# Weight splits and modulation products in instructions of 512 columns in place of 1024, in a kernel of four transformer blocks

## The chip, the cores and the metric

The kernel runs on one core of one Trainium2 chip. The metric is the device time of one execution in microseconds; the kernel before takes 1881.81 us, the median of three runs (1880.52 to 1883.42). The profile is of one more execution.

## The reference

Two models follow each other on one sequence of 512 tokens of width 1024, all in fp32, each of two layers. Each layer of both takes shift, scale and gate columns from a condition vector (the modulation), normalises the tokens, multiplies them with an input projection, mixes, multiplies with an output projection and adds the gated result; the second model has a wide MLP behind that.

```python
def modulation(cond, w_mod, b_mod):
    m = jax.nn.silu(cond) @ w_mod + b_mod
    return jnp.split(m, 3, axis=-1)
# first model: layer 0 pool mixer + attention, layer 1 Hyena convolutions + Fourier mixer
    h = rmsnorm(x, norm_g[i]) * (1 + scale) + shift
    ...
    x = x + gate * y
# second model, each of two layers l
    mod = cond @ w_mod[l] + b_mod[l]
    sh1, sc1, gt1, sh2, sc2, gt2 = [m[:, None, :] for m in jnp.split(mod, N_MOD, axis=-1)]
    h = rms_norm(x, norm_g[l, 0]) * (1.0 + sc1) + sh1
    y = mixer_block(h, ...)          # short conv, sparse attention, gated linear attention, gMLP
    x = x + gt1 * rms_norm(y, norm_g[l, 1])
    h = rms_norm(x, norm_g[l, 2]) * (1.0 + sc2) + sh2
    y = jnp.square(jax.nn.relu(h @ w_up[l])) @ w_down[l]
    x = x + gt2 * rms_norm(y, norm_g[l, 3])
```

## The kernel before, in words

Tokens lie along the columns: the state xT is 8 tiles of 128 features by 512 tokens and stays in SBUF. A projection with fp32 accuracy is made of three fp32r products: every operand is split in a part hi (rounded to fp32r by ScalarE) and a part lo (the rest, subtracted on VectorE), and mm3 (line 811) multiplies hi by hi, hi by lo and lo by hi into one PSUM bank.

**Weights.** wblock (line 795) brings in a block of 256 output columns: for each half of the contraction one DMA of 128x1024 (four k tiles of 256 columns side by side) into a ring of three "raw" tiles, one copy on ScalarE into hi and one subtraction on VectorE into lo, out of a ring of eight "wh" tiles, which makes four pairs. The first projection of the second model has blocks of other widths too (272, 268 and 128 columns, so tiles of 1088, 1072 and 512). Most blocks of the up projection go another way, winograd_fm (line 963), with splits of 512 columns of its own.

**Modulation.** All but two of the modulation vectors (16 of 1024 numbers) are made on VectorE by mod_cols (line 1159): the transposed weights come in as eight 128x1024 tiles in a ring of two ("mraw"); each is multiplied with the condition's row ("crow", the same on all partitions) and summed along the columns by one instruction into one column of the result. The profile shows such a product as CUSTOM_DVE_ANT_0 with a read-out of the sum, DVE_READ_ACCUMULATOR2_ANT, behind it. A generator "mods" hands these out between blocks; need(n) (line 1282) asks for them at the latest. The first two vectors ("m0", line 1240) come from TensorE at the start.

**Seams.** Where one projection ends and a norm must be known before the next begins, cross (line 926) works by halves of the tokens: the last output tiles ("tail"), the sums of squares, the reciprocal roots by rsqrt (line 1039, nine steps of two columns on VectorE, tiles "sa", twice in a sandwich of two norms), their broadcast by TensorE, the new input's tiles hi and lo by make_h (line 1126) on VectorE, ScalarE and POOL, and the first tiles of the next projection ("head"). There are such seams at L0out/L1norm, L1out/finN/nsa 0, wo/sand1/mlp in both layers, and mlp 0/sand2 0/nsa 1.

**Order.** Nothing is issued as it is written. Plan records each operation with its engine, a cost, the phase (pl.ph, such as "nsa 1" or "L1f") and its dependences, found from ranges of rows and columns of each buffer (record, line 202; box, line 110). schedule (line 298) then places all operations by a list: time after time it takes the engine and the ready operation that can start first, and among those that can start at that time on an engine the one with the greatest priority o.bl. That is made of the due time, counted back from TensorE's order, and a bias of the phase, in us (SCHED, line 30). wins limits, for a pool ("pg" pages of SBUF, "ps" banks of PSUM) and a phase, how far ahead of the oldest unfinished user a buffer may be taken, in us of TensorE's work; lead does the same for "mods". Some additions may go to VectorE or POOL as there is room. All transfers are issued by the SP queue in the order that the list gives. Every engine then runs its own list in order; emit (line 551, with the call at line 564) writes the instructions out, which is why nearly all rows have line 564, and are told apart by tile names.

Of the kernel before, what the change touches and what calls it, by code (L numbers as in the profile page):

```python
# [10 lines left out]
F32 = mybir.dt.float32  # L11
F32R = mybir.dt.float32r
I32 = mybir.dt.int32
AF = mybir.ActivationFunctionType
OP = mybir.AluOpType
# [2 lines left out]
P = 128  # L18
S = 512
HV = (slice(0, 256), slice(256, 512))  # L20
GA, GB, GC = 9,12,15
MY = 4
NF = 2
# [29 lines left out]
    },  # L53
    bias={
        "": -15, ("SP", "L1out"): 8, ("SP", "m0"): -30, "L0 gemm 0": -8, "L0 gemm 2": -8, "L0norm": 20,
        "L0out": -15, "L0q": 106, "L1 gemm 0": 265, "L1 gemm 1": 22, "L1f": 68, "L1norm": 270, "L1out": -7,
        "conv 0": 8, "ctx": 8, "end": 170, "finN": 67, "gla 1": -15, "gla chain 0": -32, "gla chain 1": -38,
        "gmlp 0": -15, "gmlp 1": -8, "gmlp chain 0": 30, "gmlp chain 1": 40, "head 0": 75, "head 4": 15,
        "hyena chain 1": 30, "hyena chain 2": 82, "mlp 0": -8, "mlp 1": -253, "mods": -45, "nsa 0": 8,
        "sand1 1": 8, "sand2 0": 210,  # L60
    },
)
D = 1024
# [88 lines left out]
class Plan:  # L152
# [145 lines left out]
    def schedule(self):  # L298
# [11 lines left out]
        if self.prio is None:  # L310
            t = 0.0
# [11 lines left out]
            for o in ops:  # L323
                o.bl = -self.prio[o.idx]
        for o in ops:
            o.bl += self.bias.get(o.ph, 0.0) + (self.bias.get(("SP", o.ph), 0.0) if o.eng == "SP" else 0.0)
        live = {p: np.zeros(n + 1, np.int32) for p in self.pools}
        for b in {id(b): b for o in ops for b in o.bufs}.values():
            live[b.pool][b.first:b.last + 1] += b.need
# [14 lines left out]
        pos, t = [], 0.0  # L344
# [94 lines left out]
        while left:  # L439
            pick, ps = None, 1e18  # L440
            top = max((o.bl for e in names[:4] for o in ready[e] if o.deps), default=0.0)
            for e in names:
# [10 lines left out]
                for o in pool:  # L453
# [9 lines left out]
                    if any(b.slot is None for b in o.bufs):  # L463
                        q = slots(o)
# [17 lines left out]
                if bs < ps:  # L482
                    pick, ps, pe = b, bs, e
# [4 lines left out]
            if pick is None:  # L488
                o = ops[front]
# [3 lines left out]
            o, e, s = pick, pe, ps  # L493
# [41 lines left out]
            for i in o.succ:  # L535
                q = ops[i]
# [171 lines left out]
def tile_two_blocks(ctx: ExitStack, tc: tile.TileContext, a, out):  # L708
# [48 lines left out]
    def small(n, dt=F32, tag=None):  # L757
        t = pl.alloc("sa" if n <= 16 else "sb", n)
        return t if dt == F32 else t.bitcast(dt)


    V, A, G, T = (pl.engs[n] for n in ("DVE", "ACT", "POOL", "PE"))
# [32 lines left out]
    def wblock(w, c0, nkt=KT, r0=0):  # L795

        name, l = w
        off, wd = IN_AT[c0] if name == "w_in_2" else (0, 256)
        hl = []
        for hh in range(r0 // 4, (r0 + nkt) // 4):  # L800
            src, hi, lo = wraw()[:, :4 * wd], wsplit().bitcast(F32R)[:, :4 * wd], wsplit().bitcast(F32R)[:, :4 * wd]
            if name == "w_in_2":
                D_(src, a[name][l, off + hh * 4 * P * wd:off + (hh + 1) * 4 * P * wd].rearrange("(p n) -> p n", p=P))
            else:
                D_(src, a[name][l, c0 // 256, hh])
            A.activation(hi, src, AF.Copy)
            V.tensor_sub(lo, src, hi.bitcast(F32))
            hl.append(tuple(t.rearrange("p (k n) -> p k n", k=4) for t in (hi, lo)))
        return hl

# [345 lines left out]
    crow = keep([P, D], "crow")  # L1156
    mraw = ring("mraw", 2, D)

    def mod_cols(i, dst):

        old, pl.ph = pl.ph, "mods"
        for t in range(KT):
            raw = mraw()
            D_(raw, a["wmT"][i, t])
            V.tensor_tensor_reduce(raw, raw, crow, 1.0, 0.0, OP.mult, OP.add, accum_out=dst[:, t:t + 1])
            if t % MY == MY - 1:
                pl.ph = old
                yield
                old, pl.ph = pl.ph, "mods"
        pl.ph = old  # L1170


# [69 lines left out]
    m0 = keep([P, 16, 2], "m0")  # L1242
    for j in range(2):
        pa = [mmt(), mmt()]
        for k in range(KT):
            for hh in range(2):
                raw = pg()
# [5 lines left out]
        ps = axt()  # L1253
# [228 lines left out]
    for gi in range(4):  # L1482
        o = (gi % 2) * 64
# [277 lines left out]
    for i in range(2):  # L1761
        fc = pg()
        D_(fc, a["cst_fchan"][:, i * S:(i + 1) * S])
        ps = axt()
# [14 lines left out]
    for m in range(2):  # L1779
# [6 lines left out]
        qs, yd = pg(), pg()  # L1786
# [584 lines left out]
    for l in range(2):  # L2371
# [5 lines left out]
        st, head = nsa_head(l, W, act)  # L2377
# [11 lines left out]
        t = convmix(l, W, act)  # L2389
# [115 lines left out]
    for j in range(4):  # L2505
        gr.append(hp())
        ps = axt()
# [71 lines left out]
```

## Time and profile before

| | |
|---|---|
| median of three runs | 1881.81 us |
| the profiled execution | 1881.66 us |
| its span, first to last instruction | 1879.8 us |
| TensorE (PE) busy, matmuls | 1815.2 us, 97% |
| VectorE (DVE) busy | 1548.7 us, 82% |
| ScalarE (ACT) busy | 1017.0 us, 54% |
| GpSimd (POOL) busy | 194.4 us, 10% |
| mean granted TensorE clock | 0.991 |
| HBM traffic | 129 GB/s over the span |

The page gives each engine's busy time, then the groups of instructions by tile names and shape. A window row gives the same for a stretch of time. A wait is idle time of an engine, put down to the instruction that ended it. In names of tiles, "raw" is a weight tile as loaded, "wh" a split one, "sa" a small tile of up to 16 columns, "pg" any page of 512 columns, "ps" a PSUM bank.

### The profile page before, as it was taken

The numbers are of one execution on the slowest core, as the hardware profiler recorded it, in microseconds if no ns is written. First come the engines' busy times: TensorE is split into PE (matmuls) and PEld (weight loads), VectorE is DVE, ScalarE is ACT, GpSimd is POOL, SyncE is SP. The second block draws the span as 40 slices with busy tenths as digits, with TensorE's granted clock in tenths as the row PEclk, the third lists the DMA queues.
The fourth block names the chain that finished last, engine by engine and source line by source line (L and its number), as shares of the span: only waits on it lengthen the run. The fifth ranks groups of instructions, "written<-read, shape, count | busy, mean of one in ns | idle before, by whom it ended". The sixth has DMA issues, their size and how long they took to land. (4 is left out here: it accounts for less than half of the span.)

```text
span 1879.8 us, 33476 instructions
## 1 busy us (share of the span) xinstructions
PE 1815.2 (97%) x12451; PEld 1630.2 (87%) x12451; DVE 1548.7 (82%) x3453; ACT 1017.0 (54%) x2100; POOL 194.4 (10%) x204
## 2 busy tenths in 40 slices
PE   5999999999999999999999999989999999999997
PEld 2798879988988988778888889988977889999997
DVE  6687997978998699787999867799968799766777
ACT  5565674543334566564664444575656457444455
POOL 0100000000221011011210000022201130000000
PEclk9999999999999999999999999999999999999999
DMA  7627443356433356311257422243541124222221
GB/s 235 224 79 241 146 141 113 112 176 223 156 120 124 111 174 213 113 46 46 79 168 233 160 102 101 91 160 126 181 155 41 50 79 147 101 91 101 102 90 68
DMA packets 92467, 245.29 MB, mean 130 GB/s; under 512 B 10443, under 2 KB 29167, under 8 KB 92048
## 3 DMA queue, kind: packets, MB, share of 16 engines
q1 hardware_dynamic: 92304, 243.15, 38.5%
q8 instruction: 98, 1.61, 0.4%
q14 instruction: 65, 0.53, 0.1%
HBM read 234.73 MB, written 8.39 MB: 129 GB/s over the span
## 5 line engine op out<-in xcount | busy, mean ns | idle before, releaser
L564 PE MATMUL ps<-pg,wh 128*128 128x256 f32 (+1 forms) x6336 | 1108.3, 328 | 7.4 <-ACT pg L564 4.7
L564 PEld LDWEIGHTS ps<-pg,wh 128*128 128x128 f32 x6336 | 919.1, 189 | 108.6 <-ACT pg L564 7.0
L564 PE MATMUL ps<-wh,pg 128*128 128x256 f32 (+2 forms) x2976 | 378.8, 283 | 5.0 <-ACT pg L564 5.0
L564 ACT ACTIVATE wh<-raw 128x1024 fp32r<-128x1024 f32 (+3 forms) x280 | 257.7, 923 | 231.6 <-PE ps L564 223.7
L564 PEld LDWEIGHTS ps<-wh,pg 128*128 128x128 f32 x2976 | 364.5, 189 | 8.8 <-ACT pg L564 6.1
L564 DVE TENSOR_TENSOR wh<-raw,wh 128x1024 fp32r<-128x1024 f32 (+3 forms) x280 | 297.7, 1066 | 66.7 <-ACT wh L564 51.5
L564 DVE TENSOR_TENSOR pg<-pg 128x256 f32<-128x256 f32 (+4 forms) x671 | 317.3, 508 | 37.6 <-ACT pg L564 33.3
L564 ACT ACTIVATE pg<-pg 128x256 f32<-128x256 f32 (+4 forms) x628 | 274.4, 472 | 128.3 <-DVE pg L564 75.0
L564 PE MATMUL ps<-pg 128*128 128x256 f32 (+7 forms) x1560 | 235.6, 300 | 7.5 <-DMA pg<-in_hy_w_dram 2.9
L564 DVE TENSOR_TENSOR pg<-pg,ps 128x256 f32<-128x256 f32 (+1 forms) x404 | 182.9, 473 | 59.7 <-PE ps L564 55.9
L564 PEld LDWEIGHTS ps<-pg 128*128 128x128 f32 (+4 forms) x1560 | 199.8, 184 | 33.8 <-issue 7.9
L564 POOL TENSOR_TENSOR pg<-pg 128x512 f32<-128x512 f32 (+4 forms) x96 | 114.7, 1199 | 908.9 <-ACT pg L564 488.0
L564 ACT ACTIVATE pg<-ps 128x512 fp32r<-128x512 f32 (+4 forms) x212 | 104.9, 524 | 116.2 <-PE ps L564 91.5
L564 DVE TENSOR_TENSOR pg<-ps,pg 128x512 f32<-128x512 f32 (+8 forms) x278 | 146.1, 561 | 26.1 <-ACT pg L564 20.6
L564 DVE CUSTOM_DVE_ANT_0 mraw<-mraw,crow 128x1024 f32<-128x1024 f32 x128 | 155.8, 1222 | 11.2 <-DMA mraw<-in_wmT_dram 11.2
L564 ACT ACTIVATE wh<-w 128x512 fp32r<-128x512 f32 x112 | 70.3, 630 | 127.3 <-PE ps L564 103.0
L564 ACT COPY pg<-ps 128x256 f32<-128x256 f32 (+5 forms) x184 | 78.3, 438 | 99.6 <-PE ps L564 96.9
L564 DVE TENSOR_TENSOR wh<-w,wh 128x512 fp32r<-128x512 f32 x112 | 77.0, 688 | 31.7 <-PE ps L564 19.5
L564 PE MATMUL ps<-ident,pg 128*128 128x128 f32 (+1 forms) x529 | 82.8, 276 | 5.0 <-ACT pg L564 1.8
L564 PEld LDWEIGHTS ps<-ident,pg 128*128 128x128 f32 (+1 forms) x529 | 63.1, 143 | 17.7 <-ACT pg L564 5.9
L564 ACT ACTIVATE pg<-ps,sa 128x512 f32<-128x512 f32 (+3 forms) x112 | 60.6, 553 | 28.8 <-DVE sa L564 27.0
L564 PE MATMUL ps<-pg,w 128*128 128x256 f32 (+1 forms) x408 | 68.0, 284 | 1.4 <-DVE pg L564 1.4
(138 smaller groups left out, 1127.1 us busy)
## 6 DMA issues: line engine op xcount, KB each, us to landing
mraw<-in_wmT_dram SPq DMA_DIRECT2D x128, 512.0 KB, 4.2
raw<-in_w_up_dram SPq DMA_DIRECT2D x64, 512.0 KB, 3.3
raw<-in_w_down_dram SPq DMA_DIRECT2D x64, 512.0 KB, 3.2
raw<-in_w_in_dram SPq DMA_DIRECT2D x32, 512.0 KB, 3.8
raw<-in_od_w_in_dram SPq DMA_DIRECT2D x28, 512.0 KB, 3.5
raw<-in_ev_w_in_dram SPq DMA_DIRECT2D x20, 512.0 KB, 4.1
pg<-in_w_dram SPq DMA_DIRECT2D x32, 256.0 KB, 4.3
raw<-in_w_o_dram SPq DMA_DIRECT2D x16, 512.0 KB, 3.2
```

Of the source, the lines that this page charges most:

```text
L564: o.fn(*[r(v) for v in o.args], **{k: r(v) for k, v in o.kw.items()})
```

## The change

The split of a weight block and the product of the modulation are each issued as two instructions over half of the columns. The products write two partial columns, and one addition of 128x8 for each modulation vector puts them together. Beside that, the list's parameters differ: a bias may be given for an engine and a phase together, on any engine (before, on SP alone), and some values are others.

```diff
+HV2 = (slice(0, 512), slice(512, 1024))
...
     wins={
-        ("pg", "sand1 0"): 100
+        ("pg", "sand1 0"): 60
+        ("pg", "x"): 60
-        ("ps", "hyena chain 2"): 40
+        ("ps", "hyena chain 2"): 200
...
     bias={
+        ("DVE", "m0"): 8
+        ("PE", "L1f"): -30
-        "L1f": 68
+        "L1f": 53
-        "gla chain 0": -32
+        "gla chain 0": -17
+        "nsa 1": 120
...
-            o.bl += self.bias.get(o.ph, 0.0) + (self.bias.get(("SP", o.ph), 0.0) if o.eng == "SP" else 0.0)
+            o.bl += self.bias.get(o.ph, 0.0) + self.bias.get((o.eng, o.ph), 0.0)
...
-            A.activation(hi, src, AF.Copy)
-            V.tensor_sub(lo, src, hi.bitcast(F32))
+            for q in range(2):
+                qs = slice(2 * wd * q, 2 * wd * q + 2 * wd)
+                A.activation(hi[:, qs], src[:, qs], AF.Copy)
+                V.tensor_sub(lo[:, qs], src[:, qs], hi[:, qs].bitcast(F32))
...
+        part = small(16).rearrange("p (q t) -> p q t", q=2)
         for t in range(KT):
             raw = mraw()
             D_(raw, a["wmT"][i, t])
-            V.tensor_tensor_reduce(raw, raw, crow, 1.0, 0.0, OP.mult, OP.add, accum_out=dst[:, t:t + 1])
+            for q in range(2):
+                V.tensor_tensor_reduce(raw[:, HV2[q]], raw[:, HV2[q]], crow[:, HV2[q]], 1.0, 0.0, OP.mult, OP.add,
+                                       accum_out=part[:, q, t:t + 1])
...
+        V.tensor_add(dst, part[:, 0], part[:, 1])
```

## Rows read from the trace of the kernel before

**Rows 1.** The page, part 1: busy us, share of the span, instructions

```profile
PE 1815.2 (97%) x12451; PEld 1630.2 (87%) x12451; DVE 1548.7 (82%) x3453; ACT 1017.0 (54%) x2100; POOL 194.4 (10%) x204
```

**Rows 2.** Windows: us, busy (count) of PE, PEld, DVE, ACT, POOL; clock, DMA, GB/s

```profile
0.00:45.00 45.00, 26.11 (x79) 9.15 (x80) 29.38 (x71) 21.52 (x44) 2.19 (x7) 0.92 0.72 237
200.00:300.00 100.00, 95.25 (x607) 83.35 (x606) 97.77 (x236) 71.18 (x163) 7.76 (x8) 1.00 0.44 143
900.00:1000.00 100.00, 94.93 (x589) 84.16 (x588) 97.73 (x214) 61.69 (x122) 18.00 (x21) 0.98 0.39 130
1240.00:1290.00 50.00, 39.58 (x301) 37.72 (x299) 49.20 (x155) 30.04 (x72) 18.44 (x25) 0.90 0.21 71
1500.00:1600.00 100.00, 96.77 (x807) 95.23 (x806) 95.46 (x236) 62.52 (x132) 15.48 (x20) 1.00 0.33 112
```

**Rows 3.** TensorE's waits, 45 to 1860 us: total, times, longest

```profile
PE ps L564 <- ACT pg L564: 16.6, 16, 2.2
PE ps L564 <- DVE sa L564: 10.2, 7, 5.6
PE ps L564 <- DVE wh L564: 1.8, 2, 1.4
```

**Rows 4.** Timeline of PE: start, length, what, and in brackets the wait before

```profile
901.96 0.40 PE L564 MATMUL ps<-ident,sa 128*128 128x128 f32 x2 [0.70 <-DVE sa L564]
...
1263.74 0.69 PE L564 MATMUL ps<-ident,sa 128*128 128x128 f32 x2 [5.61 <-DVE sa L564]
1266.67 4.84 PE L564 MATMUL ps<-wh,pg 128*128 128x256 f32 x22 [2.23 <-ACT pg L564]
...
1531.40 0.40 PE L564 MATMUL ps<-ident,sa 128*128 128x128 f32 x2 [1.12 <-DVE sa L564]
```

**Rows 5.** Timeline of DVE in the same three places

```profile
896.19 1.23 DVE L564 TENSOR_TENSOR wh<-raw,wh 128x1024 fp32r<-128x1024 f32 x1
...
897.87 1.22 DVE L564 TENSOR_TENSOR wh<-raw,wh 128x1024 fp32r<-128x1024 f32 x1
...
1257.54 1.26 DVE L564 TENSOR_TENSOR wh<-raw,wh 128x1072 fp32r<-128x1072 f32 x1
...
1259.26 1.26 DVE L564 TENSOR_TENSOR wh<-raw,wh 128x1072 fp32r<-128x1072 f32 x1
...
1526.36 1.21 DVE L564 TENSOR_TENSOR wh<-raw,wh 128x1024 fp32r<-128x1024 f32 x1
1527.50 0.16 DVE L564 TENSOR_SCALAR sa<-sa 128x2 int32<-128x2 int32 x1
1527.57 1.22 DVE L564 TENSOR_TENSOR wh<-raw,wh 128x1024 fp32r<-128x1024 f32 x1
1528.70 0.15 DVE L564 TENSOR_TENSOR sa<-sa 128x2 f32<-128x2 f32 x1
```

**Rows 6.** Groups by shape: count, busy us, mean ns of one, idle before

```profile
L564 DVE TENSOR_TENSOR wh<-raw,wh 128x1024 fp32r<-128x1024 f32 x184 | 226.8, 1236 | 46.7 <-ACT wh L564 44.3 <-ACT pg L564 1.2 <-PE ps L564 0.2
L564 DVE TENSOR_TENSOR wh<-raw,wh 128x512 fp32r<-128x512 f32 x88 | 60.9, 693 | 20.0 <-PE ps L564 12.8 <-ACT wh L564 7.2
L564 DVE CUSTOM_DVE_ANT_0 mraw<-mraw,crow 128x1024 f32<-128x1024 f32 x128 | 155.8, 1222 | 11.2 <-DMA mraw<-in_wmT_dram 11.2
L564 DVE DVE_READ_ACCUMULATOR2_ANT m<- 128x1 f32 x128 | 10.4, 81 | 0.0
L564 ACT ACTIVATE wh<-raw 128x1024 fp32r<-128x1024 f32 x184 | 193.8, 1057 | 126.2 <-PE ps L564 118.9 <-DMA raw<-in_w_in_dram 4.2 <-DMA raw<-in_ev_w_in_dram 1.9
L564 ACT ACTIVATE wh<-raw 128x512 fp32r<-128x512 f32 x88 | 55.1, 626 | 102.9 <-PE ps L564 102.9
```

**Rows 7.** Timeline of DVE: a 512-column split and its successor

```profile
8.62 0.69 DVE L564 TENSOR_TENSOR pg<-pg 128x512 fp32r<-128x512 f32 x1
9.23 0.42 DVE L564 SCALAR_TENSOR_TENSOR pg<-pg 128x256 f32<-128x256 f32 x1
```

More of the change, by code (lines that the diff above doesn't have):

```diff
@@ L41 @@
         ("pg", "mlp 1"): 200, ("pg", "mods"): 60, ("pg", "nsa 0"): 80, ("pg", "nsa 1"): 40,
[11 rows of a table removed]
[12 rows of a table added]
     },
     bias={
[L55 to L60, printed above, removed]
[3 rows of a table added]
+        "gla chain 0": -17, "gla chain 1": -38, "gmlp 0": -15, "gmlp 1": -8, "gmlp chain 0": 30,
+        "gmlp chain 1": 40, "head 0": 75, "head 4": 15, "hyena chain 1": 30, "hyena chain 2": 82,
+        "mlp 0": -8, "mlp 1": -253, "mods": -45, "nsa 0": 8, "nsa 1": 120, "sand1 1": 8, "sand2 0": 210,
     },
```

26 rows, old and new, of tables (bias, wins) are left out of this document.

## The prediction

> **What bounds the kernel now.** I read the page first [rows 1]: TensorE is busy for 1815.2 of the 1879.8 us and VectorE for 1548.7, so TensorE sets the time and its idle 64.6 us are all that another engine's change can win. Then the windows [rows 2] show where those lie. The first 45 us hold 18.9 of them, while the first weights come in. Of the rest the four stretches listed, 350 us long, hold 23.5 (4.7, 5.1, 10.4, 3.2), and in just these VectorE is busy for 340.2 us, 97%. There the matmuls have caught up with a chain of small VectorE steps (the reciprocal roots of a norm, two columns wide), and everything else that VectorE has to do stands between those steps. Then TensorE's waits from 45 to 1860 us [rows 3]: 16.6 us for ScalarE's tiles, 10.2 for the small VectorE columns ("sa"), and for weight splits 1.8. The timeline shows what makes the "sa" waits long [rows 4, 5]. At 1526.36 a whole weight split goes in between two steps of the chain, the next step begins at 1527.50, a second split follows at 1527.57, the step after it is at 1528.70, and TensorE, which wants the result, stands for 1.12 us. The same pair of splits sits at 896 to 898, ahead of a wait of 0.70, and at 1257 to 1260, ahead of one of 5.61, the longest of the "sa" waits.
>
> **The change part by part.** The sum is made against the profiled execution, 1881.66 us (span 1879.8 and 1.9 around it); the median of the runs is 1881.81, 0.15 more.
>
> *Instructions added.* Splits in halves: 184 of 128x1024 [rows 6] and, by the list of parts in the code, 4 each of 1088, 1072 and 512 columns, so 196 on each of ScalarE and VectorE; 128 more products and, with each, one more read-out; 16 small adds. No transfer and no matmul is added.
>
> *Their cost on VectorE.* By durations two halves cost 2 x 693 - 1236 = 150 ns more than the whole [rows 6], 29 us for 196. But instructions overlap: a 1024 split keeps the engine for 1.14 us before the next begins [rows 5], a 512 one for 0.61 (8.62 to 9.23) [rows 7], so a pair costs 0.08 us more, 16 us in all. No product of 512 columns is in the trace. The nearest row is again the split (1222 against 1236 ns whole): 0.08 more each, 10 us; the upper end is by durations, with the read-out of 81 ns [rows 6] in full: 2 x (693 + 81) - (1222 + 81) = 245 ns, 31 us. Sixteen adds at the 0.15 of a small step [rows 5] are 2.4. VectorE gets 28 to 62 us more and has 331 idle [rows 1]; a gain there is excluded, since the columns stay and the instructions double. Beside the matmuls this is hidden, and that cover is gone only in the full stretches. Seven waits on "sa" [rows 3], with four split instructions taken for the full run ahead of each (the two seen, and two more for what stands earlier), at 0.08: **+2.2**. Ends: 0, and 19% (350 of 1880) of 62, that is 11. I take a value near the low end because TensorE is 93% busy even in these stretches.
>
> [...]
>
> *Their cost on ScalarE.* 2 x 626 - 1057 = 195 ns [rows 6] x 196 = 38 us at most, on an engine busy for 1017 us [rows 1]. Its idle time hides them: **0** (ends 0 and, for 16 waits [rows 3] behind one pair each, 3).
>
> *Shorter stops in the chain.* With halves, a step of the chain waits for 0.61 and not 1.14: 0.53 us less per split, two splits for each of the three waits shown, but no more than the wait: 0.70 + 1.06 + 1.06 = **-2.8**. Ends: 0, if the second half goes into the next gap in place of a shorter filler, and 0.70 + 2.28 + 1.12 = -4.1, if both splits leave the chain. What is late next is ScalarE's tile of the normed input, made behind that chain (2.23 us at 1266.67 [rows 4]).
>
> *ScalarE behind a whole copy.* It spends 194 of its 1017 us [rows 1, 6] in the copies; a wanted tile finds one running 19% of the time and then waits half of 1057 or of 626 ns: 0.19 x 0.215 x 16 waits = **-0.7** (ends 0 and -3).
>
> *First half of a block earlier.* The planner notes column ranges, so matmuls of k 0 and 1 need only the first halves. Two waits for splits, 1.8 us [rows 3], lose about half a split each: **-1.1** (ends 0 and -1.8).
>
> *The products.* A whole one holds the engine for about as long as a split, and none of them stands between the small steps in the rows read here: **0** (ends 0 and, one whole product out of each of seven waits at 0.53, -3.7). The modulation columns come one small add later (0.15), which nobody was seen waiting for.
>
> [...]
>
> *Order.* The lists move too. "nsa 1" gets 120 us of priority on all engines, its loads on SP among them, so its weight splits and projections stand ahead of the last products of "mlp 0", whose rows make the chain: ScalarE, VectorE and POOL queue the other work behind. "L1f" loses 15 and on TensorE 30 more, "gla chain 0" gains 15, the small steps of "m0" gain 8 on VectorE, "hyena chain 2" may take PSUM banks further ahead, "sand1 0" pages less far; the "x" entry equals the default. A lower priority delays the matmuls of "L1f" and whatever evicts them. The trace doesn't show these orders. Bounds: they can win at most the 10.4 us idle in 1240 to 1290 [rows 2], and a new wait as long as the longest there loses 5.6 [rows 4]. The four splits of "nsa 1" have little room elsewhere (four pairs of buffers), so I take **-2**.
>
> Sum: 2.2 - 2.8 - 0.7 - 1.1 - 1.5 - 2 = -5.9, so 1881.7 - 5.9, about **1876 us**. Chance 0.42, own range 1871 to 1878.
>
> **The rivals.** *No change*: both halves are ready together and nearly as urgent, so they run back to back and the chain waits as before, or the change doesn't do what it says because a reader waits for the whole tile anyway. For it: at 1526 two whole splits went into two gaps in a row [rows 5], so two halves may fill the same two gaps and the other two the next. Against it: in the first two gaps alone that already saves 1.06, which is lost again only if the later gaps were otherwise empty. Then +2.2 and the orders' own share: 1880 to 1884; chance 0.22.
>
> *Slower*: VectorE becomes the bound in the four full stretches. The place is the norm between two projections, the price the 19% share of 28 to 62 us, 5 to 11, say 8 with nothing won: **1890**. It decides if VectorE's queue in those stretches never empties before TensorE's wait, so that each added 0.08 to 0.25 us is passed on whole. For it: 97% busy there. Against it: TensorE waits more for ScalarE than for "sa", and the splits can go earlier. Chance 0.20. [...]
>
> *Much faster*: the new order takes the splits at 1257 to 1260 [rows 5] away, the 5.61 us wait closes and the clock stays high. Idle 10.4 and clock 5 of that stretch [rows 2] come back: about 1866. Against it: buffers. Chance 0.16.
>
> **How the numbers follow.** A measurement here tells about 0.2%, 3.8 us, from no change: 1878.0 to 1885.6. Faster is the forecast and the last rival, 0.58; same 0.22; slower 0.20. The range reaches from somewhat below the last rival's middle to the slower rival's price, 1863 to 1890, and leaves out some 4% below and 8% above. The forecast and the last rival have the same sign.
>
> **What would show it.** Right: splits of 128x512 with 196 x 2 on both engines, 256 products at about 0.69 us, VectorE busy about 1575 us (1610 by durations), and "sa" waits of TensorE down from 10.2 to about 7 us with single halves between the small steps. The bound by VectorE would show as longer waits on "sa" and ScalarE's tiles in the full stretches; the no-change case as halves in direct succession and the same waits. The order's term is wrong if the wait near 1260 moves or grows with the splits of "nsa 1" already done. The forecast falls if the waits elsewhere grow by more than these shrink.

## The result, and the profile after

| | before | after |
|---|---|---|
| median | 1882.9 us, 5 runs (1880.52 to 1883.72) | 1898.44 us, 5 runs (1893.4 to 1901.97) |
| ratio, with its 95% interval | | 1.0074 [1.0056, 1.0092] |
| the profiled execution, its span | 1881.66, 1879.8 us | 1893.4, 1891.6 us |
| mean granted TensorE clock | 0.991 | 0.987 |

The change makes the kernel slower, by 0.56 to 0.92%. The forecast was 1876 us, the range 1863 to 1890: wrong in sign, and outside the range.

The page of the kernel after, part 1, against [rows 1]:

```profile
PE 1822.1 (96%) x12451; PEld 1637.9 (87%) x12451; DVE 1570.5 (83%) x3920; ACT 1047.1 (55%) x2297; POOL 188.5 (10%) x205
```

VectorE has 21.8 us more, ScalarE 30.1, where 28.4 (by the pitch of the rows) and at most 38 were forecast. The span has grown by 11.8: 6.9 of it stand as TensorE's busy time (the same 12451 matmuls, longer ones) and 4.9 as its idle time. The profiled execution is the shortest of the five, so its rows hold 11.8 of the 15.5 us by which the medians differ. The groups by shape, against [rows 6]:

```profile
L566 DVE TENSOR_TENSOR wh<-raw,wh 128x512 fp32r<-128x512 f32 x452 | 304.8, 691 | 90.5 <-ACT wh L566 66.0 <-PE ps L566 17.8 <-ACT pg L566 5.5
L566 ACT ACTIVATE wh<-raw 128x512 fp32r<-128x512 f32 x452 | 276.2, 628 | 240.0 <-PE ps L566 234.9 <-DMA raw<-in_ev_w_in_dram 2.7 <-DMA kf<-pg 0.4
L566 DVE CUSTOM_DVE_ANT_0 mraw<-mraw,crow 128x512 f32<-128x512 f32 x256 | 173.3, 695 | 6.4 <-DMA mraw<-in_wmT_dram 6.1
```

The change does what it says: splits of 512 columns (452 = 84 that were there and 368 new ones; before, 88 stand in that row, 4 of them the narrow blocks that are halved now), and 256 products of 695 ns, about the 0.69 us foretold. TensorE's waits from 45 to 1860 us, against [rows 3]:

```profile
PE ps L566 <- ACT pg L566: 16.9, 19, 2.5
PE ps L566 <- DVE pg L566: 14.3, 19, 2.8
PE ps L566 <- DVE sa L566: 8.3, 5, 6.0
```

The second row is the one that matters. The same view of the kernel before has it too, and the prediction left it out; no single wait in it is longer than 0.7 us:

```profile
PE ps L564 <- DVE pg L564: 6.3, 15, 0.7
```

Waits for pages written by VectorE went from 6.3 to 14.3 us, while "sa" lost 1.9 and the row for weight splits (1.8) is gone. The longest "sa" wait is still where it was, before the last norm of "mlp 0". Timeline of PE, after, against [rows 4]:

```profile
356.29 4.90 PE L566 MATMUL ps<-pg,wh 128*128 128x256 f32 x28 [2.79 <-DVE pg L566]
...
1269.32 0.69 PE L566 MATMUL ps<-ident,sa 128*128 128x128 f32 x2 [6.04 <-DVE sa L566]
1272.30 3.95 PE L566 MATMUL ps<-wh,pg 128*128 128x256 f32 x16 [2.29 <-ACT pg L566]
```

And VectorE's timeline in the same two places, against [rows 5]:

```profile
353.06 2.49 DVE L566 TENSOR_TENSOR wh<-raw,wh 128x512 fp32r<-128x512 f32 x4
355.47 2.48 DVE L566 TENSOR_TENSOR pg<-ps,pg 128x512 f32<-128x512 f32 x4
...
1261.29 0.70 DVE L566 TENSOR_TENSOR wh<-raw,wh 128x536 fp32r<-128x536 f32 x1
1261.91 0.15 DVE L566 TENSOR_TENSOR sa<-ps,sa 128x2 f32<-128x2 f32 x1
...
1262.57 1.29 DVE L566 TENSOR_TENSOR wh<-raw,wh 128x536 fp32r<-128x536 f32 x1
1263.78 0.14 DVE L566 TENSOR_TENSOR sa<-sa,ps 128x2 f32<-128x2 f32 x1
...
1264.24 0.70 DVE L566 TENSOR_TENSOR wh<-raw,wh 128x536 fp32r<-128x536 f32 x1
1264.87 0.15 DVE L566 TENSOR_SCALAR sa<-sa 128x2 f32<-128x2 f32 x1
1264.94 0.70 DVE L566 TENSOR_TENSOR wh<-raw,wh 128x536 fp32r<-128x536 f32 x1
1265.57 0.15 DVE L566 TENSOR_SCALAR sa<-sa 128x2 int32<-128x2 int32 x1
```

At 1261 to 1265 the halves stand between the small steps, as foretold, and each step does wait for 0.63 us (1264.24 to 1264.87) in place of 1.14. But the four halves of the two splits take one gap after the other, as the end of that term had it, and one of them lasts 1.29 us in place of 0.70 (1262.57; the last section comes back to it). TensorE's stop is no shorter: 6.04 us against 5.61. At 353 the four halves run in direct succession ahead of the pages that TensorE wants, and it stands for 2.79 us. That stop is the largest new one, and it took the place of the 1.36 us for a split at 353.50 of the kernel before. Right behind it the granted clock falls. Columns as in [rows 2], after, then before:

```profile
356.00:359.00 3.00, 2.71 (x13) 2.74 (x14) 3.00 (x8) 2.82 (x6) 0.73 (x1) 0.50 0.84 274
353.00:359.00 6.00, 5.50 (x46) 5.50 (x47) 6.00 (x14) 3.88 (x8) 0.00 (x0) 1.00 0.51 177
```

The clock's records in the two traces hold two levels, 0.50 and 1.00. At 0.50 matmuls of 256 columns begin 0.21 us apart here, at 1.00 (360 to 362 us) 0.12. By these records the clock stands at the lower level for 52.9 us after and for 34.3 before, and TensorE is busy for 39.4 and 20.3 us of that; at 0.21 in place of 0.12 the difference costs an estimated 8 us. By that estimate the 6.9 us of busy time that TensorE has gained are no added work, but the clock. One execution of each doesn't tell how much of that is the change's: the granted clock of the five runs after is 0.982 to 0.987, and that of the 97 runs of the kernel before that were measured beside the experiments 0.983 to 0.992.

The stretch of 300 to 400 us, and that from 800 to 900, are the two in which TensorE's busy time fell most (2.5 and 3.0 us), and neither was among the full ones. Windows of the kernel after, columns as in [rows 2]:

```profile
300.00:400.00 100.00, 96.10 (x691) 90.48 (x690) 89.81 (x205) 54.12 (x104) 8.06 (x9) 0.98 0.44 134
800.00:900.00 100.00, 94.04 (x596) 78.81 (x595) 79.37 (x196) 53.27 (x113) 10.73 (x12) 0.98 0.15 49
```

The kernel before:

```profile
300.00:400.00 100.00, 98.64 (x706) 92.35 (x705) 80.73 (x166) 51.72 (x88) 7.43 (x8) 1.00 0.37 119
800.00:900.00 100.00, 97.01 (x629) 82.67 (x628) 80.14 (x192) 55.14 (x106) 14.76 (x13) 0.98 0.14 48
```

### The profile page after: what moved, and what is told of

It reads as the page before. It is cut to its first block, busy times and chain, and to the rows that moved or that the text cites. A ratio compares the mean times of both kernels' runs of the same rounds, so it can differ in the third digit from the quotient of the medians.

```text
span 1891.6 us, 34203 instructions
## 1 busy us (share of the span) xinstructions
PE 1822.1 (96%) x12451; PEld 1637.9 (87%) x12451; DVE 1570.5 (83%) x3920; ACT 1047.1 (55%) x2297; POOL 188.5 (10%) x205
## 4 chain that ended last, share of the span: by engine, by line
PE 79%; DVE 14%; ACT 3%; issue 2%; DMA 1%; SPq 0%; POOL 0%; DVEq 0%; ACTq 0%; POOLq 0%
PE ps L566 79%; DVE pg L566 9%; ACT pg L566 3%; DVE sa L566 2%; DVE wh L566 2%; DVE mraw L566 1%; DMA mraw<-in_wmT_dram 0%; ACT wh L566 0%; DMA pg<-in_cst_filt_dram 0%; SPq L566 0%; DVE xT L566 0%; POOL pg L566 0%; ACT L566 0%; DVE w L566 0%; DVE sb L566 0%
## 5 line engine op out<-in xcount | busy, mean ns | idle before, releaser
L566 ACT ACTIVATE wh<-raw 128x512 fp32r<-128x512 f32 (+1 forms) x476 | 288.9, 626 | 246.3 <-PE ps L566 241.0
L566 DVE TENSOR_TENSOR wh<-raw,wh 128x512 fp32r<-128x512 f32 (+1 forms) x476 | 319.1, 688 | 90.6 <-ACT wh L566 66.0
L566 PE MATMUL ps<-pg 128*128 128x256 f32 (+8 forms) x1560 | 232.1, 300 | 6.3 <-DMA pg<-in_hy_w_dram 2.9
L566 PEld LDWEIGHTS ps<-pg 128*128 128x128 f32 (+5 forms) x1560 | 198.2, 185 | 30.8 <-DVE pg L566 5.8
L566 POOL TENSOR_TENSOR pg<-pg 128x256 f32<-128x256 f32 (+4 forms) x93 | 102.7, 1111 | 941.1 <-ACT pg L566 438.3
L566 DVE CUSTOM_DVE_ANT_0 mraw<-mraw,crow 128x512 f32<-128x512 f32 x256 | 173.3, 695 | 6.4 <-DMA mraw<-in_wmT_dram 6.1
L566 DVE TENSOR_TENSOR pg<-ps,pg 128x512 f32<-128x512 f32 (+8 forms) x278 | 146.2, 561 | 20.1 <-ACT pg L566 16.6
```

Of the source, the lines that this page charges most:

```text
L566: o.fn(*[r(v) for v in o.args], **{k: r(v) for k, v in o.kw.items()})
```

## The experiments

Theory **instructions**: VectorE's added time reaches the path wherever its work is placed just in time, full stretch or not. Theory **order**: the new windows and biases, and the list that is planned with halves, are worse than the old list. Every ratio is to the kernel before, measured beside it on the same chip.

### The halves alone, in the old order

**e1** leaves the list of the kernel before as it is and issues each split and product as two halves in direct succession, at the place of the whole one. The products sum into a fixed tile, and one small add follows the eighth.

```diff
-            o.fn(*[r(v) for v in o.args], **{k: r(v) for k, v in o.kw.items()})
+            args, kw = [r(v) for v in o.args], {k: r(v) for k, v in o.kw.items()}
+            (o.parts or o.fn)(*args, **kw)
...
             A.activation(hi, src, AF.Copy)
+            pl.ops[-1].parts = lambda hi, src, f, wd=wd: [
+                nc.scalar.activation(hi[:, q:q + 2 * wd], src[:, q:q + 2 * wd], f) for q in (0, 2 * wd)]
...
```

The subtraction and the product get parts of their own in the same way.

> The kernel before with its list of operations and its order on every engine unchanged, but each of the 196 weight splits and 128 products issued as two halves in direct succession (392 copies, 392 subtractions, 256 products, 16 additions). Theory 'instructions': the fixed cost of the added instructions on VectorE makes the loss; with 324 more at 0.07 to 0.16 us it is 1890 to 1900 us, and TensorE's waits on VectorE grow. Theory 'order': the added instructions are hidden and only the new order loses; 1881 to 1886 us, VectorE's busy time up by some 25 us and TensorE's waits as before.

Measured: 1896.2 us, 1.0055 [1.0036, 1.0073]. The page and TensorE's waits from 45 to 1860 us:

```profile
PE 1823.1 (96%) x12451; PEld 1631.2 (86%) x12451; DVE 1575.8 (83%) x3921; ACT 1036.9 (55%) x2296; POOL 190.1 (10%) x204
```

```profile
PE ps L565 <- ACT pg L565: 17.3, 17, 2.2
PE ps L565 <- DVE sa L565: 12.1, 10, 5.8
PE ps L565 <- DVE pg L565: 11.9, 24, 1.1
PE ps L565 <- DVE wh L812: 0.9, 1, 0.9
```

Halves in an unchanged order make up most of the loss, and without a single long stop: 24 waits for VectorE's pages, the longest 1.1 us. Since the order is the same, each matmul can be set against itself in the trace of before. Three of them are those of [rows 4], 6.75, 9.96 and 14.24 us later here. Timeline of PE, e1:

```profile
908.71 0.41 PE L565 MATMUL ps<-ident,sa 128*128 128x128 f32 x2 [0.90 <-DVE sa L565]
...
974.76 10.51 PE L565 MATMUL ps<-pg,wh 128*128 128x256 f32 x81 [0.96 <-DVE pg L565]
...
1273.70 0.69 PE L565 MATMUL ps<-ident,sa 128*128 128x128 f32 x2 [5.77 <-DVE sa L565]
...
1545.64 0.40 PE L565 MATMUL ps<-ident,sa 128*128 128x128 f32 x2 [1.59 <-DVE sa L565]
```

Worked out so for all matmuls, the delay grows by 15.5 us from 45 to 1860. (That is by one execution of each, and e1's is the longest of its five; the ratio says 10.4, so take what follows as shares.) Of that the four stretches of [rows 2] hold 5.2 (1.7, 2.0, 0.5, 1.1), two stretches in which the clock stands at its lower level for longer than before 3.2 (near 820 us, where the granted clock is 0.91 from 810 to 830 against 1.00, and near 1465), and all the rest 7.1. From 1060 to 1245, where TensorE is busy without a break and VectorE for 132.4 of 185 us, it doesn't grow at all. The matmul at 974.76, 966.77 in the trace of before, began there 0.12 us after the one ahead of it; now it stands for 0.96.

**e7** and **e8** do the same for the weight splits alone and for the products alone.

> As e1, but only the weight splits in halves. By VectorE's added time (14 of 25 us) some 5 to 7 us over before, 1889 to 1893 us; if the products alone make the loss, 1883 to 1887.

> As e1, but only the products in halves. By VectorE's added time (9 to 12 of 25 us) some 4 to 5 us over before, 1888 to 1891 us; if the weight splits alone make the loss, 1883 to 1887.

Measured: splits 1889.44 us, 1.0029 [1.0017, 1.0042]; products 1891.29 us, 1.0034 [1.0016, 1.0053]. The two make up e1's 0.55 within the intervals, and both parts of the change cost. **e10** halves only ScalarE's copies in place, **e11** only VectorE's subtractions.

> The list and its order are those of the kernel before; only ScalarE's 196 copies of the splits are issued as two halves in direct succession, VectorE's subtractions stay whole. Both kinds of split together gave 1.0029 in place. If VectorE's added time makes that: 0.999 to 1.001 here, and TensorE's waits for ScalarE's tiles stay at 16 to 17 us. If ScalarE's 0.09 us more per pair (18 us in all) counts as much as VectorE's: 1.0015 to 1.003, with those waits longer by 2 us or more.

> The counterpart: only VectorE's 196 subtractions are issued as two halves in direct succession, ScalarE's copies stay whole. VectorE gets about 14 us more. If its time is what passes to the path at 0.4 to 0.5 of itself: 5.5 to 7 us, 1.002 to 1.004, with waits on small VectorE steps up from 6 to about 8 us. If ScalarE's part made the 1.0029: 0.999 to 1.001.

Measured: copies 1883.88 us, 1.0007 [0.9996, 1.0018]; subtractions 1886.56 us, 1.0014 [0.9998, 1.0031]. ScalarE's waits in e10 stay at 15.7 us, so its halves cost nothing that can be told from zero. The subtractions came out below their expectation, and neither interval excludes no change; only both together (e7) do.

**e6** issues quarters of 256 columns in place, e1's edit with four parts.

> As e1, but four quarters of 256 columns in direct succession: three added instructions in place of one, the order of before. Theory 'instructions': VectorE gets three times the 27 us of e1, and the loss is two to three times its 10 us, 1905 to 1920 us. Theory 'order' (the 10 us of e1 come from a run's spread or from something that doesn't grow with the count): 1890 to 1900 us.

Measured: 1938.5 us, 1.029 [1.0266, 1.0314]; the page, and the waits:

```profile
PE 1849.8 (95%) x12451; PEld 1648.8 (85%) x12451; DVE 1629.1 (84%) x4841; ACT 1077.5 (56%) x2688; POOL 188.7 (10%) x204
```

```profile
PE ps L565 <- DVE pg L565: 25.5, 33, 2.8
PE ps L565 <- ACT pg L565: 19.1, 21, 2.2
PE ps L565 <- DVE sa L565: 14.8, 9, 6.0
```

Three times e1's time on VectorE (80.4 us against 27.1) costs five times as much, with VectorE still idle for 311 us: more than the two to three times that were expected.

**e9** goes the other way: the old order, each product over the first 512 columns alone.

```diff
...
+    def first_half(o, x, y, *a, accum_out):
+        nc.vector.tensor_tensor_reduce(o[:, :S], x[:, :S], y[:, :S], *a, accum_out=accum_out)
...
+            pl.ops[-1].parts = first_half
```

> The list and its order are those of the kernel before; each of the 128 products reads only the first 512 of its 1024 columns, so that half of each modulation sum is left out. VectorE loses about 128 x 0.53 = 68 us, the other engines nothing. Theory 'VectorE's time is on the path in both directions' (halves of the products in place added 13 us of it and passed on 0.34% of the time, that is 6 us, 0.45 of it): between -0.25 and -0.45 of 68, so 17 to 30 us less, ratio 0.984 to 0.991, with all three of TensorE's waits (ScalarE's tiles, small VectorE columns, small VectorE steps) shorter. Theory 'the order is fitted to the durations': delays cost, gains do not, since what comes next on VectorE waits for TensorE anyway: ratio 0.996 to 1.000.

Measured: 1881.3 us, 0.9977 [0.9961, 0.9992]. The page and the waits:

```profile
PE 1821.4 (97%) x12451; PEld 1636.9 (87%) x12451; DVE 1487.2 (79%) x3453; ACT 1016.0 (54%) x2100; POOL 189.5 (10%) x204
```

```profile
PE ps L565 <- ACT pg L565: 15.0, 15, 2.2
PE ps L565 <- DVE sa L565: 7.9, 5, 5.6
PE ps L565 <- DVE pg L565: 4.9, 13, 0.7
```

So VectorE's time is not on the path in both directions. (In this profile TensorE is idle for 6.2 us less than before and busy for 6.2 more, at a granted clock of 0.986; over all runs the clock is 0.987, against 0.988 beside it.) Set side by side, the us of the path being the ratio's excess times 1882:

| run, old order | VectorE busy | path, us [interval] | share passed on |
|---|---|---|---|
| e9, half of each product | -61.5 | -4.3 [-7.3, -1.5] | 0.07 |
| e11, subtractions in halves | +13.4 | +2.6 [-0.4, 5.8] | 0.19 |
| e7, splits in halves | +14.1 | +5.5 [3.2, 7.9] | 0.39 |
| e8, products in halves | +14.0 | +6.4 [3.0, 10.0] | 0.46 |
| e1, both | +27.1 | +10.4 [6.8, 13.7] | 0.38 |
| e6, both in quarters | +80.4 | +54.6 [50.1, 59.1] | 0.68 |

Less work on VectorE gives back next to nothing, more work is passed on in good part, and the more of it the larger the part: this fits an order in which most of VectorE's instructions end shortly before TensorE asks for them, though how long before was not measured. (e7 and e1 add ScalarE's halves too, which e10 puts at 1.3 us, not told apart from nothing. e6 adds ScalarE's quarters, 60.5 us of its time, and no run tells their share of the 54.6.)

### The order

**e3** has the new windows and biases with whole instructions; **e2** both splits, planned with the old ones; **e4** the products alone in halves, planned with the old ones.

> The new windows and biases with whole splits and products. Theory 'parameters': all of the loss is here, 1893 to 1902 us. Theory 'instructions': as before, 1880 to 1885 us. Theory 'order' (any list that differs from the fitted one loses some): between, 1885 to 1895 us.

> Both splits of the change, placed by the list, with all parameters (windows, biases) as before. Theory 'order': the halves placed one by one change the order and lose as much as the whole change or more, 1893 to 1908 us, since the other parameters were not fitted to the halves. Theory 'instructions': the same as two halves in direct succession, within 4 us. Theory 'parameters' (the loss comes from the new biases and windows): 1878 to 1886 us.

> The products of the modulation alone in halves, the weight splits whole, all parameters as before. If the products make the loss by the list: 1890 us or more; if the weight splits do, 1881 to 1886 us here.

Measured: e3 1893.64 us, 1.0043 [1.0021, 1.0064]; e2 1900.87 us, 1.0082 [1.0056, 1.0107]; e4 1895.68 us, 1.0055 [1.0038, 1.0071]. The new parameters lose without any halves, and planning the halves is no better than issuing them in the old places: e2 against e1 0.82 to 0.55, e4 against e8 0.55 to 0.34, though the intervals overlap.

The granted clock goes with this. With the halves in the old places its mean over the runs is that of the kernel before beside them (e1 0.989, e7 0.989, e8 0.988, against 0.989, 0.988, 0.988); with planned halves it is lower (e2 0.984, e4 0.983, against 0.989). Among the 97 runs of the kernel before a clock lower by 0.001 goes with about 1 us more. By that the lower clock of e2 and e4 is an estimated 4 to 6 us, as much as they lie behind e1 and e8 (5.1 and 4.0). That the re-planned order brings the clock down by its stops is argued; no run separates the two.

e3's waits are 17.1 us for ScalarE's tiles, 13.2 for "sa" and 8.1 for VectorE's pages: less of the last than in e1, more of the second.

**e12** is the changed kernel once more, beside e9 to e11.

> The changed kernel on the same chip and beside the same runs of the kernel before as the in-place kernels. If the new order and the new parameters win nothing net over the same halves issued in the old order (1.0055): 1.0055 to 1.009. If the first comparison put it too high because it ran on another chip, and the planning does win back part of the halves' cost: below 1.004.

Measured: 1895.18 us, 1.006 [1.004, 1.008]. It stands with the first comparison and beside e1: new order and new parameters together leave 0.05 to 0.2% on top of the halves, within the intervals nothing. They win nothing.

**e5** takes the order of the changed kernel and issues whole instructions in it: for each pair of halves one whole one at the place of the first, where what it reads is there, or else of the second. That could be done for all 128 products, 190 of the 196 subtractions and 134 of the 196 copies.

> The changed kernel with its own order on every engine, but 128 of 128 pairs of products, 190 of 196 pairs of subtractions and 134 of 196 pairs of copies issued as one whole instruction again, at the place of the pair's first half where all that it needs is there by then, else of the second. Theory 'instructions': most of the loss goes with them, 1882 to 1889 us. Theory 'order': the loss stays, 1892 us or more.

Measured: 1923.48 us, 1.0208 [1.0183, 1.0233]; VectorE is busy for 1553.9 us, about as in e3 (1553.0), and TensorE's waits are:

```profile
PE ps L595 <- DVE pg L595: 25.7, 33, 3.3
PE ps L595 <- ACT pg L595: 18.1, 17, 2.5
PE ps L595 <- DVE sa L595: 12.2, 7, 6.2
```

Neither theory foresaw this: "instructions" is refuted, and "order", which holds by its 1892 us or more, had the loss stay, not grow. With 17 us less of VectorE's work than the changed kernel it is 1.3 to 1.5% slower. A whole instruction in the first half's place brings the second half forward by as much, ahead of work that TensorE wants; that this is the cause is argued, and how much the 62 copies left in halves add is not known. It says that the order can count for more than the sum of busy time.

**e13** and **e14** take e3 apart: the 120 us for "nsa 1" alone, and all the others (among them one that the section on the change doesn't list: a bias of -15 us for operations without a phase is gone). **e15** and **e16** keep the old parameters and move three biases each by 3 us that have nothing to do with the change:

```diff
e15
-        ... "mlp 0": -8, "mlp 1": -253, "mods": -45, "nsa 0": 8,
+        ... "mlp 0": -8, "mlp 1": -253, "mods": -45, "nsa 0": 5, "nsa chain 0": 3, "sand1 0": 3,
e16
-        ... "gla 1": -15, ...
+        ... "gla 1": -12, "gla 0": 3, "L0kv": -3, ...
```

> Whole instructions; of the new parameters only the 120 us of priority for the second layer's phase nsa 1. The new parameters together gave 1.0043. If that one large move makes the loss: 1.003 to 1.005, and the waits around 1250 to 1300 longer. If any other order loses some: 1.001 to 1.003. The prediction's order term, which was put down to this move: 0.998 to 0.999.

> The counterpart: all the new parameters but the 120 us for nsa 1, whole instructions. If nsa 1 made the loss: 0.999 to 1.001. If any other order loses some: 1.002 to 1.004.

> Whole instructions and the old parameters, with three priorities of the middle of layer 0 moved by 3 us that have nothing to do with the change; the order differs from about 570 us on. If the old order was fitted by measurement and any other order loses, as much as the new parameters do for no reason of their own: 1.002 to 1.006. If the new parameters are bad by themselves: 0.999 to 1.001 here.

> As the run before, with three other priorities moved by 3 us (gla 1 from -15 to -12, gla 0 by 3, L0kv by -3); the order differs from the first weights on. Any other order loses: 1.002 to 1.006. The new parameters are bad by themselves: 0.999 to 1.001.

Measured: e13 1890.51 us, 1.0042 [1.0023, 1.006]; e14 1894.24 us, 1.0056 [1.0034, 1.0079]; e15 1881.88 us, 1.0005 [0.9989, 1.0021]; e16 1891.12 us, 1.0044 [1.003, 1.0058]. Each half of the new parameters loses as much as all of them; an arbitrary nudge loses as much again, and another one nothing (in e15 TensorE's order differs only from 685 us on, in e16 from 49). So the loss needs neither the "nsa 1" move nor these parameters: of five other orders with whole instructions four lose 0.42 to 0.56% and none wins. That the old order had been picked by measured times would explain it, but is only argued. Where e16 loses, its waits don't tell; they differ from those of before by little (17.7, 8.7, 7.4 us for ScalarE's tiles, "sa" and "pg"). In the profiles of e16 and e13 TensorE is idle for 64.3 and 63.5 us, no longer than before (64.6), and all the growth stands as its busy time, at a clock of 0.989 and 0.987. Over all their runs the clock is lower by 0.001 and 0.003 than beside them, which by the same estimate makes 1 and 3 of their 8 us; the rest stays open.

### The products and GpSimd

In e1 some halves of a product last 1.77 us and not 0.68. Timeline of DVE there, ahead of the wait at 974.76, and of POOL:

```profile
971.52 0.67 DVE L1169 CUSTOM_DVE_ANT_0 mraw<-mraw,crow 128x512 f32<-128x512 f32 x1
972.13 0.07 DVE L1169 DVE_READ_ACCUMULATOR2_ANT mpart<- 128x1 f32 x1
972.13 1.77 DVE L1169 CUSTOM_DVE_ANT_0 mraw<-mraw,crow 128x512 f32<-128x512 f32 x1
973.84 0.07 DVE L1169 DVE_READ_ACCUMULATOR2_ANT mpart<- 128x1 f32 x1
```

```profile
971.14 2.22 POOL L565 TENSOR_TENSOR pg<-pg 128x512 f32<-128x512 f32 x1 [36.98 <-DVE pg L565]
```

GpSimd's addition stands at 971.14 to 973.36 and needs 1.30 us by itself (the median of GpSimd's 70 operations on 512 columns in the trace of before): it seems to wait for the first half to end (972.13) and to run then, and the second half, there since 972.13, to wait for it in turn, 1.09 us. In the kernel before the same product is a whole one, and what follows reads PSUM and isn't held up while the same addition runs (964.12 to 966.87). Ten us later it is a weight split that follows a product, and that takes 2.30 us in place of 1.22. DVE, then POOL, of the kernel before:

```profile
964.50 1.22 DVE L564 CUSTOM_DVE_ANT_0 mraw<-mraw,crow 128x1024 f32<-128x1024 f32 x1
...
965.64 1.21 DVE L564 TENSOR_TENSOR pg<-pg,ps 128x256 f32<-128x256 f32 x3
...
974.12 1.22 DVE L564 CUSTOM_DVE_ANT_0 mraw<-mraw,crow 128x1024 f32<-128x1024 f32 x1
...
975.27 2.30 DVE L564 TENSOR_TENSOR wh<-raw,wh 128x1024 fp32r<-128x1024 f32 x1
```

```profile
964.12 2.75 POOL L564 TENSOR_TENSOR pg<-pg 128x512 f32<-128x512 f32 x1 [36.87 <-DVE pg L564]
974.35 2.14 POOL L564 TENSOR_TENSOR pg<-pg 128x512 f32<-128x512 f32 x1 [7.47 <-DVE pg L564]
```

So halving puts a second instruction that reads SBUF twice right behind the first, where something harmless stood before. Behind products there are three such stalls before (at 736.65, 975.27 and 1359.19) and six in e1, e8 too, and the two largest steps by which e1's matmuls fall behind (1.1 us at 966.77, 0.9 at 1357.74 of the kernel before) lie at them. Halves of splits meet it as well: in e1 three second halves take 1.22 or 1.23 us in place of 0.69 (820.63, 823.72, 1527.34), beside additions of 256 columns. **e17** and **e18** shorten those of GpSimd's 128x512 operations that work in place, without and with the products in halves; seven eighths of their columns are left out:

```diff
+            if o.eng == "POOL" and len(o.args) > 1 and o.args[0] is o.args[1] and all(tuple(getattr(v, "shape", ())) == (P, S) for v in args):
+                args = [v[:, :S // 8] for v in args]
```

> The kernel before, in which GpSimd's operations on 128x512 that work in place do only the first 64 columns (seven eighths of each are left out), list and order unchanged. In the trace a VectorE instruction next to a product lasts 1.09 us longer where such an operation runs, and ends with it (three times in the kernel before, six with the products in place). Alone this should give 0.997 to 1.000: three stalls of VectorE are gone, and the old order was not short of their time.

> The same with the products as halves in direct succession. Products in place gave 1.0034 against the kernel before. If the meetings with GpSimd make two thirds of that, this stands at 1.001 above the run before it, 1.0015 at most; if it is the halves' own 0.07 us each, and the small adds and read-outs, 1.002 to 1.004 above it.

Measured: e17 1881.36 us, 0.9992 [0.9982, 1.0003]; e18 1885.43 us, 1.0014 [1.0002, 1.0026]. The stalls behind products are gone: no half of a product in e18 is longer than 0.90 us, and at the place shown above the timeline of DVE, and then that of POOL, has

```profile
968.37 0.81 DVE L1167 CUSTOM_DVE_ANT_0 mraw<-mraw,crow 128x512 f32<-128x512 f32 x1
```

```profile
967.38 1.25 POOL L567 TENSOR_TENSOR pg<-pg 128x64 f32<-128x64 f32 x1 [35.34 <-DVE pg L567]
```

So the meeting with GpSimd is what stretched them. (A split at 1068.68 of e17, beside an addition of 128x512 that was left whole, still takes 1.98 us in place of 1.22.) The products' halves still cost 0.22% (1.0014 over 0.9992) of the 0.34, as the second of the two expectations has it; but the intervals of both runs, 0.1% to either side, don't exclude the first's 0.15, so the share of the meetings, a third by the middles, is not settled.

## Why the prediction was wrong, step by step

**Their cost on VectorE (+2.2): the term that failed.** The size of the added work was right: 28.4 us by the pitch of the rows, 27.1 measured in e1; the 62 us by durations is excluded. What failed is "beside the matmuls this is hidden, and that cover is gone only in the full stretches", with seven waits of four splits each. That let 8% of the 28.4 us pass on, and e1 measured 38%, 10.4 us. The four stretches hold a third of the growth. The prediction read VectorE's cover off its busy share (331 us idle), and looked for late work only in rows with long waits; the row of 15 waits of at most 0.7 us for VectorE's pages was a sign that much else is finished just in time, and it is the one that grew (6.3 to 14.3).

**Their cost on ScalarE (0)**: right, 1.3 us in e10 with an interval that holds 0.

**Shorter stops in the chain (-2.8)**: the end named "0, if the second half goes into the next gap" is what happened at 1261 to 1265; the longest wait is 6.04 against 5.61. "sa" did fall from 10.2 to 8.3 in sum, but whole instructions in other orders give 7.4 (e15) to 13.2 (e3), so the halves have no claim to it.

**ScalarE behind a whole copy (-0.7)**: not seen, 16.9 us against 16.6. Its 19% is the copies' share of ScalarE's busy time; a wanted tile would find one running 10% of the time (194 of 1880 us), which halves the term. **First half of a block earlier (-1.1)**: the wait for splits is gone after, and 0.9 of 1.8 in e1, which was the right size; but after, a longer wait for pages took its place at 356.

**The products (0)**: wrong, 6.4 us in e8. They were taken off the sum because none stood between the small steps; by the middles two thirds of their cost come by the added time, placed elsewhere, and some perhaps by the meeting with GpSimd, which the trace of before showed and the prediction didn't look for.

**Clock (-1.5)**: no run shows this term. The stretch 1240 to 1290 has a granted clock of 0.90 as before (10.24 us of it at 0.50 in both traces), and the long wait ahead of it stayed. What the runs showed in its place is the lower level behind new stops as well, as at 356: in the profiles 52.9 us of it after, 34.3 before, an estimated 8 us lost where 1.5 were to be won. How much of that is the change's and how much differs from run to run anyway is open; e1, whose clock over its runs is that of the kernel before, has its 10.4 us without it.

**Order (-2)**: the sign was wrong. The new parameters by themselves cost 0.43%, 8 us, and "nsa 1", on which the term rested, 0.42% alone. The two seem not to add: 0.55 and 0.43 would be 0.98, and the changed kernel has 0.60 to 0.74, though with 0.2 to either side of each the intervals nearly meet. What makes a re-planned order lose stays open.

**The rivals.** *Slower* came nearest, 1890 with a chance of 0.20, and it was right that added VectorE time reaches the path. That its 8 us lie near e1's 10.4 is partly luck: it had the added time passed on whole in the four full stretches and not at all elsewhere, while the four hold a third of the growth and 38% was passed on over all. VectorE was at 82% and others waited for it, and breaking its instructions up still cost 0.55% in place (e1). *Much faster* asked that the splits at 1257 to 1260 go away; the 6.04 us wait stayed. *No change* asked for the old waits; those for pages doubled.

## What to carry to other kernels

Idle time of an engine is not slack (in e6 VectorE is idle for 311 us, and 54.6 us are lost). In a list that places work just in time, added time is passed on at once (here 0.4 of it) while removed time gives next to nothing back (0.07), so count the short waits of the busy engine for it, not only the long ones, before you write down "hidden". Smaller instructions help a waiting chain only if the scheduler leaves the gap empty; one that fills gaps puts the other half in (here 6.04 us of wait against 5.61). And a re-planned order is a draw (here four of five lost): measure it with the old instructions first, and against a nudge that means nothing. Where TensorE's busy time grows with the same matmuls, look at the granted clock behind each new stop (here 0.50 from 356 to 359 us).

## What was not expected of the hardware

In these traces VectorE and GpSimd hold each other up, and halves made more of it. GpSimd's additions of 128x512 next to a product took 2.14 to 2.75 us in place of 1.30, and VectorE's next instruction with two operands in SBUF 1.03 to 1.11 us longer (three times before, six in e1), while one that reads PSUM ran beside them (in the trace of before 305 such instructions overlap a GpSimd operation with two inputs, and none lasts 0.4 us longer than the median of its shape). With those additions cut to 64 columns VectorE's stalls behind products were gone, while GpSimd still took 1.25 us at 967.38, where others of that size take 0.32. In the kernel after, the half split at 1262.57, 1.29 us in place of 0.70, has GpSimd's additions of 256 columns beside it (1261.43 to 1263.28). Why the two engines hold each other up, no run shows, and the rows give no rule for who goes first: by the records the addition stands since 964.12, and the product that begins at 964.50 still takes its usual 1.22 us, ahead of it.

The read-out of a sum (0.07 us) overlaps wholly with what follows: in e1 the next product begins at the same 972.13.
